# Longer matmul runs in a two-layer transformer trunk: an up projection in runs of 512 columns, a down projection laid out by tokens, and activation slots shifted by 64 and 128 bytes

## The chip, the cores and the metric

The kernel runs on one core of a Trainium2 chip. The metric is the device time of one execution in microseconds (us), lower is better. Engines are named as in the profile: PE (matmul) and PEld (its weight loads), DVE, ACT, POOL, and SP, which issues nearly all DMAs.

## The reference, cut to what matters

Two decoder layers over 256 tokens of width 1024, in float32. The attention half of a layer is a combined projection, three kinds of attention heads, gates and an output projection. The half that the change touches is the MLP at the end of each layer:

```
h = rmsnorm(x, norm_mlp)
x = x + jnp.square(jax.nn.relu(h @ w_up)) @ w_down      # w_up 1024 x 4096, w_down 4096 x 1024
```

After the second layer one more rmsnorm gives the output.

## The kernel before, in words

**Precision.** Every float32 operand of a projection is split into a high part, rounded to the matmul type fp32r, and a low part, the rest. A product a*b is then three matmuls: low weight by high activation, high weight by high activation, high weight by low activation. Weights come as 280 pieces of 128 x 1024 (140 a layer), each by one DMA of 512 KB into a ring `raw` (4 buffers). `split_one` makes the high part (`wh`, ACT, L118) and the low part (`wl`, DVE, L119), six buffers each. `split(n)` also starts the next three pieces, at high priority.

**Layout.** The residual `xres` lies with channels on partitions, [128, 8, 256]: eight channel tiles of 256 tokens. `hilo_slot` gives a 16 KB slot from two that take turns, [128, 2, 8, 256]: eight high tiles, then eight low tiles. It serves as normalized input (`hl`, `xh`), attention output (`oT`) and gated sum (`mg`). `norm_split` (L158 on ACT, L159 on DVE) fills one channel tile of a slot from `xres`; `sumsq` adds its square for the norm. The norm's factor per token is applied after the projections: in the MLP as its square, since relu squared lets it pass through.

**Projection.** `proj` makes 24 matmuls for a 128-wide output tile: for each of eight channel tiles the three products, 256 columns (tokens) each, weights stationary (L198, L199, L200). `v_chunk`, the first work of a layer, is laid out the other way: tokens stationary, 512 weight columns moving (L243 to L245).

**MLP.** 32 hidden tiles of 128 are made in 16 pairs by `up_pair`: two `proj` into the halves of one PSUM bank (`mm`, two buffers), then relu (ACT, L540), square (ACT, L542), high part (DVE copy, L545), low part (DVE, L546) into slots `ga`. The program is written as: pair i of the up projection, then the down products of pair i-1. In the first layer `down(j, d)` multiplies hidden tile j into channel tile d: three matmuls of 256 columns, weights stationary (L557 to L559), for eight d, so 768 matmuls. In the second layer `down_nat(j, t, h)` is laid out by tokens: 128 tokens stationary, 512 weight columns moving, three matmuls (L583 to L585) for four groups (t, h), so 384 matmuls. Both add up in two PSUM tiles `acc2` of two banks each. The last four hidden tiles (TAIL) are kept back and done group by group, so that each group ends apart from the others and its follow-up can start.

**End of the first layer.** For each d: last products, `dve` multiplies by R2 (the squared factor, spread over partitions by `bcast`, L188, and squared at L513), adds to `xres` (L644, L645), then `norm_split` and `sumsq` for the next layer (L168). The next layer's `v_chunk` needs the channel tiles of `hl` one after the other.

**Order.** The Tile framework orders each engine's instructions by a planner that runs its own cost model over the program, so the order on PE follows the program and the priorities only roughly. Attention scores are sent to PE as closed bursts (`burst`, L283). Slots in SBUF follow one another in the order in which their names first occur. Counted from the slots' sizes, `hl`, `ga`, `wh`, `wl` and `V` all lie a multiple of 256 bytes from each other.

Of the kernel before, what the change touches and what calls it, by code (L numbers as in the profile page):

```python
# [30 lines left out]
W_BUFS = 6  # L31
# [7 lines left out]
WK = 5  # L39
# [1 line left out]
START = "w0 x0 w0 x1 w1 x2 w1 x3 w2 x4 x5 w3 x6 x7".split()  # L41
NORM_ACT = False
TAIL = 4
SKEW = 2
# [17 lines left out]
def trunk(ctx: ExitStack, tc: tile.TileContext, w, x, norms, gfin, consts, out):  # L62
# [82 lines left out]
    ident = cst["ident"]  # L145
# [3 lines left out]
    act.activation(tri, tri_raw, AF.Copy)  # L149
    negtri, negones = tri[:, 0], tri[:, 1]  # L150

    def hilo_slot():
        return T("hl", [P, 2, KT, S], 2, F32R)

    def norm_split(hl, nrm, d):

        g = cst["norms"][:, nrm, d:d + 1]
        act.activation(hl[:, 0, d], xres[:, d], AF.Copy, scale=g)  # L158
        dve.scalar_tensor_tensor(hl[:, 1, d], xres[:, d], g, hl[:, 0, d].bitcast(F32),  # L159
                                 op0=ALU.mult, op1=ALU.subtract)  # L160

    def sumsq(d, acc):
# [28 lines left out]
    def proj(dst, n, hl, nk=KT, first=True, last=True, koff=0, woff=0):  # L191

        hi, lo = split(n)
        for k in range(nk):
            c = (woff + k) * P
            a = (first and k == 0)
            z = (last and k == nk - 1)
            pe.matmul(dst, lo[:, c:c + P], hl[:, 0, koff + k], start=a, stop=False, skip_group_check=True)  # L198
            pe.matmul(dst, hi[:, c:c + P], hl[:, 0, koff + k], start=False, stop=False, skip_group_check=True)  # L199
            pe.matmul(dst, hi[:, c:c + P], hl[:, 1, koff + k], start=False, stop=z, skip_group_check=True)  # L200

    acc = T("acc", [P, S], 1)
    hl = hilo_slot()
    for d in range(KT):
        norm_split(hl, 0, d)
        sumsq(d, acc)
# [1 line left out]
    for layer in range(DEPTH):  # L208
        base = layer * PIECES
        xs = hl  # L210
        with tc.high_priority(offset=RPRI):
# [1 line left out]
            Rp = bcast(rcol)  # L213
            R = T("R", [P, S], 1)
            act.activation(R, Rp, AF.Copy)
        xh = hilo_slot()

        def normalized():

            for d in range(KT):  # L220
                t = T("sq", [P, S], 3)
                g = cst["norms"][:, 2 * layer, d:d + 1]
                dve.scalar_tensor_tensor(t, xres[:, d], g, R, op0=ALU.mult, op1=ALU.mult)
                act.activation(xh[:, 0, d], t, AF.Copy)
                dve.tensor_tensor(xh[:, 1, d], t, xh[:, 0, d].bitcast(F32), op=ALU.subtract)


        V = {}
# [1 line left out]
        def v_chunk(c, n):  # L230
            if c == 0:
                pv = [mm_bank(), mm_bank()]
            else:
                sb = s_bank()
                pv = [sb[:, 0], sb[:, 1]]
            for q in range(4):
                hi, lo = split(n + q)
                for kk in range(2):
                    k = 2 * q + kk
                    wsl = slice(kk * 512, kk * 512 + 512)  # L240
                    for t in range(2):
                        tsl = slice(t * P, t * P + P)
                        pe.matmul(pv[t], xs[:, 0, k, tsl], lo[:, wsl], start=k == 0, stop=False)  # L243
                        pe.matmul(pv[t], xs[:, 0, k, tsl], hi[:, wsl], start=False, stop=False)  # L244
                        pe.matmul(pv[t], xs[:, 1, k, tsl], hi[:, wsl], start=False, stop=k == KT - 1)  # L245
# [44 lines left out]
        oT = hilo_slot()  # L290
        last_exp = [None]
        T0, T1, TT = slice(0, P), slice(P, S), slice(0, S)

# [4 lines left out]
            dve.tensor_tensor(oF[j * DH:(j + 1) * DH], po[0:DH, 0:S], tmp, op=ALU.add)  # L298

        def o_split(oF, kt):  # L300
            last_exp[0] = act.activation(oT[:, 0, kt], oF, AF.Copy)
            dve.tensor_tensor(oT[:, 1, kt], oF, oT[:, 0, kt].bitcast(F32), op=ALU.subtract)

        def pv_mm(po, head, kt, ph, pl, first, last):

# [176 lines left out]
                act.preload_act_table_set("natural_log_exp_and_others")  # L482


        mg = hilo_slot()
        for d in range(KT):
            n = base + 60 + d
            st = s_bank()
            sf = st.rearrange("p a b -> p (a b)")
            proj(sf[:, 0:S], n, oT, nk=2, koff=0, woff=0)  # L490
            proj(sf[:, S:2 * S], n, oT, nk=3, koff=2, woff=2)
            proj(sf[:, 2 * S:3 * S], n, oT, nk=3, koff=5, woff=5)
            m3 = T("wk", [P, 3, S], WK)
            m3f = m3.rearrange("p a b -> p (a b)")
            dve.tensor_tensor(m3f, sf[:, 0:3 * S], G[d].rearrange("p a b -> p (a b)"), op=ALU.mult)
            dve.tensor_tensor(m3[:, 0], m3[:, 0], m3[:, 1], op=ALU.add)
            dve.tensor_tensor(m3[:, 0], m3[:, 0], m3[:, 2], op=ALU.add)
            act.activation(mg[:, 0, d], m3[:, 0], AF.Copy)
            dve.tensor_tensor(mg[:, 1, d], m3[:, 0], mg[:, 0, d].bitcast(F32), op=ALU.subtract)


        acc = T("acc", [P, S], 1)
        hl = hilo_slot()
# [46 lines left out]
        def down(j, d):  # L550
            hi, lo = split(npc["d", j])
            uh, ul = us[j // 2]
            a = j == 0 and d < 4
            z = j == 2 * npairs - 1
            dst = down_dst(d)
            c = slice(d * P, d * P + P)
            pe.matmul(dst, lo[:, c], uh[:, j % 2], start=a, stop=False, skip_group_check=True)  # L557
            pe.matmul(dst, hi[:, c], uh[:, j % 2], start=False, stop=False, skip_group_check=True)  # L558
            pe.matmul(dst, hi[:, c], ul[:, j % 2], start=False, stop=z, skip_group_check=True)  # L559

        last = layer == DEPTH - 1
        if last:
# [5 lines left out]
            for t in range(2):  # L568
                for h in range(2):
# [4 lines left out]
            r2 = T("rc", [P, 2], 8)  # L574
            dve.tensor_tensor(r2, rcol, rcol, op=ALU.mult)

        def down_nat(j, t, h):
            hi, lo = split(npc["d", j])
# [5 lines left out]
            pe.matmul(dst, uh[:, j % 2, k], hi[:, c], start=False, stop=False)  # L584
            pe.matmul(dst, ul[:, j % 2, k], hi[:, c], start=False, stop=j == 2 * npairs - 1)  # L585

        groups = [(t, h) for t in range(2) for h in range(2)] if last else [(d,) for d in range(KT)]
        one = down_nat if last else down
        body = 2 * npairs - TAIL
        for i in range(npairs + 1):  # L590
            if i < npairs:
# [40 lines left out]
        hl = hilo_slot()
        for d in range(KT):
            if d == 0:
                for e in range(SKEW):
                    for j in range(body, 2 * npairs - 2):
                        down(j, e)
            if d + SKEW < KT:
# [106 lines left out]
```

## Time and profile before

| what | value |
|---|---|
| time, median of 3 runs | 884.33 us (883.89 to 885.01) |
| time of the profiled execution | 884.33 us |
| its span, first to last instruction | 882.6 us |
| PE busy | 870.9 us, 99% of the span, 6648 matmuls |
| PEld busy | 833.1 us |
| DVE busy | 598.9 us, 68% |
| ACT busy | 494.2 us, 56% |
| granted clock of PE | 0.998 |

A matmul's busy time reaches past the start of the next one, so what one matmul costs in a stream is read from start to start, or from a count of them in a stretch without gaps.

### The profile page before, as it was taken

How to read it: one execution, taken by the hardware profiler on the slowest of the kernel's cores; microseconds unless marked ns; L12 is line 12 of the kernel's file. 1: busy time of each engine (PE TensorE's matmuls, PEld its weight loads, DVE VectorE, ACT ScalarE, POOL GpSimd, SP SyncE). 2: the span in 40 equal slices, each digit the busy share in tenths (PEclk: the TensorE clock that was granted, in tenths of full speed). 3: DMA queues.
4: the chain of work that ended last, by engine and by line, in shares of the span. 5: the costliest groups of instructions: out<-in, count | busy, mean ns of one | idle time of the engine just before them, and what ended most of it. 6: DMA issues, size and time to landing. Idle time of an engine off the chain costs nothing.

```text
span 882.6 us, 16351 instructions
## 1 busy us (share of the span) xinstructions
PE 870.9 (99%) x6648; PEld 833.1 (94%) x6648; DVE 598.9 (68%) x899; ACT 494.2 (56%) x732; POOL 50.7 (6%) x64
## 2 busy tenths in 40 slices
PE   8999999999999999999999999999999999999996
PEld 7899999999999999999988999999999999999995
DVE  6977878855886554555678878787567865555553
ACT  7756566758365444444466664666573554444442
POOL 3000101000030000000020101010000300000000
PEclk9999999999999999999999999999999999999999
DMA  9755443454556666666565554344554666666641
GB/s 316 258 173 159 144 143 121 155 160 151 180 181 186 187 187 181 180 188 184 151 196 187 174 162 142 122 141 146 168 167 145 214 192 191 189 190 187 189 127 48
DMA packets 43562, 151.47 MB, mean 172 GB/s; under 512 B 4960, under 2 KB 6368, under 8 KB 43488
## 3 DMA queue, kind: packets, MB, share of 16 engines
q1 hardware_dynamic: 43056, 149.90, 55.2%
q8 instruction: 52, 0.85, 0.4%
q10 hardware_dynamic: 432, 0.54, 0.2%
q14 instruction: 22, 0.18, 0.1%
HBM read 149.37 MB, written 1.05 MB: 170 GB/s over the span
## 4 chain that ended last, share of the span: by engine, by line
PE 94%; DVE 2%; DMA 1%; issue 1%; ACT 1%; SPq 0%; POOLq 0%; ACTq 0%
PE mm L198 18%; PE mm L199 18%; PE mm L200 18%; PE s L557 4%; PE s L559 4%; PE s L558 3%; PE s L583 3%; PE s L584 3%; PE s L585 3%; PE s L283 2%; PE s L198 2%; PE s L199 2%; PE s L200 2%; PE s L243 2%; PE s L245 2%; PE s L244 2%
## 5 line engine op out<-in xcount | busy, mean ns | idle before, releaser
L119 DVE TENSOR_TENSOR wl<-raw,wh 128x1024 fp32r<-128x1024 f32 (+1 forms) x282 | 343.8, 1222 | 221.7 <-ACT wh L118 221.1
L118 ACT ACTIVATE wh<-raw 128x1024 fp32r<-128x1024 f32 (+1 forms) x282 | 295.0, 1051 | 274.0 <-PE mm L200 151.1
L198 PE MATMUL mm<-hl,wl 128*128 128x256 f32 x1344 | 382.1, 285 | 1.9 <-DVE xres L507 1.9
L199 PE MATMUL mm<-hl,wh 128*128 128x256 f32 x1344 | 381.3, 284 | 0.0
L200 PE MATMUL mm<-hl,wh 128*128 128x256 f32 x1344 | 379.8, 284 | 0.0
L198 PEld LDWEIGHTS mm<-hl,wl 128*128 128x128 f32 x1344 | 257.3, 191 | 3.7 <-DVE xres L507 2.4
L199 PEld LDWEIGHTS mm<-hl,wh 128*128 128x128 f32 x1344 | 257.3, 192 | 0.9
L200 PEld LDWEIGHTS mm<-hl,wh 128*128 128x128 f32 x1344 | 256.7, 191 | 0.3 <-DVE hl L159 0.2
L557 PE MATMUL s<-ga,wl 128*128 128x256 f32 x256 | 72.6, 284 | 0.0
L558 PE MATMUL s<-ga,wh 128*128 128x256 f32 x256 | 72.4, 283 | 0.0
L559 PE MATMUL s<-ga,wh 128*128 128x256 f32 x256 | 72.2, 283 | 0.0
L169 POOL TENSOR_TENSOR acc<-acc,sq 128x256 f32<-128x256 f32 x28 | 26.9, 962 | 417.4 <-ACT sq L168 242.6
L583 PE MATMUL s<-wl,ga 128*128 128x512 f32 x128 | 50.1, 392 | 0.0
L584 PE MATMUL s<-wh,ga 128*128 128x512 f32 x128 | 50.0, 391 | 0.0
L557 PEld LDWEIGHTS s<-ga,wl 128*128 128x128 f32 x256 | 49.1, 192 | 0.4 <-DVE sq L644 0.2
L585 PE MATMUL s<-wh,ga 128*128 128x512 f32 x128 | 49.5, 389 | 0.0
L558 PEld LDWEIGHTS s<-ga,wh 128*128 128x128 f32 x256 | 49.1, 192 | 0.1
L559 PEld LDWEIGHTS s<-ga,wh 128*128 128x128 f32 x256 | 49.0, 192 | 0.2 <-DVE ga L546 0.2
L198 PE MATMUL s<-hl,wl 128*128 128x256 f32 x128 | 36.5, 285 | 0.0
L199 PE MATMUL s<-hl,wh 128*128 128x256 f32 x128 | 36.2, 283 | 0.0
L200 PE MATMUL s<-hl,wh 128*128 128x256 f32 x128 | 36.2, 283 | 0.0
L410 POOL TENSOR_SCALAR_AFFINE_SELECT wk<-wk 128x256 f32<-128x256 f32 x24 | 18.4, 790 | 221.2 <-DVE wk L422 152.2
(132 smaller groups left out, 1124.4 us busy)
## 6 DMA issues: line engine op xcount, KB each, us to landing
raw<-in_w_dram SPq DMA_DIRECT2D x278, 512.0 KB, 4.2
raw<-in_w_dram SPq DMA_DIRECT2D x4, 256.0 KB, 3.5
xres<-in_x_dram SPq DMA_DIRECT2D x8, 128.0 KB, 5.6
wk<-in_gfin_dram SPq DMA_DIRECT2D x2, 256.0 KB, 4.4
out_dram<-V SPq DMA_DIRECT2D x2, 256.0 KB, 2.3
out_dram<-V ACTq DMA_DIRECT2D x2, 256.0 KB, 2.1
c_maskA<-in_maskA_dram SPq DMA_DIRECT2D x1, 384.0 KB, 6.1
c_rope<-in_rope_dram SPq DMA_DIRECT2D x1, 256.0 KB, 5.7
```

The source lines that it names most:

```text
L118: act.activation(hi[:, c:c + step], r[:, c:c + step], AF.Copy)
L119: dve.tensor_tensor(lo[:, c:c + step], r[:, c:c + step], hi[:, c:c + step].bitcast(F32), op=ALU.subtract)
L169: pool.tensor_tensor(acc, acc, sq, op=ALU.add)
L198: pe.matmul(dst, lo[:, c:c + P], hl[:, 0, koff + k], start=a, stop=False, skip_group_check=True)
L199: pe.matmul(dst, hi[:, c:c + P], hl[:, 0, koff + k], start=False, stop=False, skip_group_check=True)
L200: pe.matmul(dst, hi[:, c:c + P], hl[:, 1, koff + k], start=False, stop=z, skip_group_check=True)
L557: pe.matmul(dst, lo[:, c], uh[:, j % 2], start=a, stop=False, skip_group_check=True)
L558: pe.matmul(dst, hi[:, c], uh[:, j % 2], start=False, stop=False, skip_group_check=True)
L559: pe.matmul(dst, hi[:, c], ul[:, j % 2], start=False, stop=z, skip_group_check=True)
L583: pe.matmul(dst, uh[:, j % 2, k], lo[:, c], start=j == 0, stop=False)
L584: pe.matmul(dst, uh[:, j % 2, k], hi[:, c], start=False, stop=False)
L585: pe.matmul(dst, ul[:, j % 2, k], hi[:, c], start=False, stop=j == 2 * npairs - 1)
```

## The change

It has four parts. (1) `hilo_slot(i)` now names its slot, and a slot lies as [128, 8, 2, 256]: of each channel tile the high and the low part side by side, 512 columns in one run. (2) `up_pair` gives each hidden tile a PSUM bank of its own and calls `proj_wide`: eight matmuls of 512 columns (high weight by high and low activation, into the two halves of the bank) and eight of 256 (low weight by high activation). A DVE reduce adds the halves; relu and square become one DVE operation; the high part moves to ACT. (3) The first layer's down projection uses `down_nat`, as the second layer does. At its end each group is scaled on ACT, transposed back by four PE transposes and added to `xres` by one DVE operation; R2 and its broadcast go. (4) The slots are named early, with fillers `skip0` to `skip2`, so that modulo 256 bytes `hl1` lies 64 and `ga` 128 bytes beyond the weights, `hl0` level with them.

```diff
+    for tag, shape, bufs, dt in (("hl0", [P, KT, 2, S], 1, F32R),
+                                 ("skip0", [P, 16], 1, F32),
+                                 ("hl1", [P, KT, 2, S], 1, F32R),
+                                 ("skip1", [P, 16], 1, F32),
+                                 ("ga", [P, 3, S], KT, F32),
+                                 ("skip2", [P, 32], 1, F32),
+                                 ("wh", [P, 1024], W_BUFS, F32R), ("wl", [P, 1024], W_BUFS, F32R), ("V", [P, 2, 8, 2, DH], 3, F32R)):
+        T(tag, shape, bufs, dt)
...
+    def proj_wide(n, hl, bank):
+
+        hi, lo = split(n)
+        for k in range(KT):
+            pe.matmul(bank, hi[:, k * P:k * P + P], hl[:, k].rearrange("p a b -> p (a b)"), start=k == 0, stop=False,
+                      skip_group_check=True)
+        for k in range(KT):
+            pe.matmul(bank[:, 0:S], lo[:, k * P:k * P + P], hl[:, k, 0], start=False, stop=k == KT - 1,
+                      skip_group_check=True)
...
-        if layer < DEPTH - 1:
-            R2 = T("tmp", [P, S], 2)
-            act.activation(R2, bcast(rcol), AF.Square)
...
         def up_pair(i):
-            p = mm_bank()
-            proj(p[:, 0:S], npc["u", 2 * i], hl)
-            proj(p[:, S:2 * S], npc["u", 2 * i + 1], hl)
-            s1 = T("wk", [P, 512], WK)
-            act.activation(s1, p, AF.Relu)
-            u = T("wk", [P, 512], WK)
-            act.activation(u, s1, AF.Square)
+            t = T("wk", [P, 2, S], WK)
+            for a in range(2):
+                p = mm_bank()
+                proj_wide(npc["u", 2 * i + a], hl, p)
+                dve.tensor_reduce(t[:, a], p.rearrange("p (a b) -> p b a", a=2), axis=mybir.AxisListType.X, op=ALU.add)
+            u = T("wk", [P, 2, S], WK)
+            dve.scalar_tensor_tensor(u, t, 0.0, t, op0=ALU.max, op1=ALU.mult)
             uh = T("ga", [P, 2, S], KT, F32R)
             ul = T("ga", [P, 2, S], KT, F32R)
-            dve.tensor_copy(uh.rearrange("p a b -> p (a b)"), u)
-            dve.tensor_tensor(ul.rearrange("p a b -> p (a b)"), u, uh.rearrange("p a b -> p (a b)").bitcast(F32), op=ALU.subtract)
+            act.activation(uh, u, AF.Copy)
+            dve.tensor_tensor(ul, u, uh.bitcast(F32), op=ALU.subtract)
...
-        groups = [(t, h) for t in range(2) for h in range(2)] if last else [(d,) for d in range(KT)]
-        one = down_nat if last else down
+        groups = [(t, h) for t in range(2) for h in range(2)] if last else [(t, h) for h in range(2) for t in range(2)]
+        one = down_nat
...
-            tmp = T("sq", [P, S], 3)
-            dve.tensor_tensor(tmp, down_dst(d), R2, op=ALU.mult)
-            dve.tensor_tensor(xres[:, d], xres[:, d], tmp, op=ALU.add)
-            norm_split(hl, 2 * layer + 2, d)
-            sumsq(d, acc)
+            y = T("wk", [P, 512], WK)
+            act.activation(y, acc2[h][:, t], AF.Copy, scale=r2[:, t:t + 1])
+            tb = t_bank()
+            for d in range(4):
+                pe.transpose(tb[:, d * P:(d + 1) * P], y[:, d * P:(d + 1) * P], ident)
+            x4 = xres[:, 4 * h:4 * h + 4, t * P:(t + 1) * P]
+            dve.tensor_tensor(x4, x4, tb.rearrange("p (a b) -> p a b", a=4), op=ALU.add)
+            if t == 1:
+                for d in range(4 * h, 4 * h + 4):
+                    norm_split(hl, 2 * layer + 2, d)
+                    sumsq(d, acc)
```

## Rows read from the trace of the kernel before

**Rows 1.** Page, part 1 and part 2: busy time by engine, clock by slice.

```profile
PE 870.9 (99%) x6648; PEld 833.1 (94%) x6648; DVE 598.9 (68%) x899; ACT 494.2 (56%) x732; POOL 50.7 (6%) x64
...
PEclk9999999999999999999999999999999999999999
```

**Rows 2.** Page, part 4: the chain that ended last, by engine.

```profile
PE 94%; DVE 2%; DMA 1%; issue 1%; ACT 1%; SPq 0%; POOLq 0%; ACTq 0%
```

**Rows 3.** Windows: the first layer's MLP, all matmuls 256 columns wide; busy (x started).

```profile
274.00:434.00 160.00, 160.00 (x1336) 160.00 (x1335) 82.19 (x83) 74.34 (x84) 0.00 (x0) 1.00 0.63 185
```

**Rows 4.** Timeline of PE, second layer: from 256 columns to 512 and back.

```profile
740.99 0.28 PE L200 MATMUL mm<-hl,wh 128*128 128x256 f32 x1
741.11 0.40 PE L583 MATMUL s<-wl,ga 128*128 128x512 f32 x1
...
742.50 0.39 PE L583 MATMUL s<-wl,ga 128*128 128x512 f32 x1
...
746.58 0.28 PE L198 MATMUL mm<-hl,wl 128*128 128x256 f32 x1
746.69 0.28 PE L199 MATMUL mm<-hl,wh 128*128 128x256 f32 x1
746.81 0.28 PE L200 MATMUL mm<-hl,wh 128*128 128x256 f32 x1
```

**Rows 5.** Chain in order of time: start, length; transposes, and R2's broadcast.

```profile
268.07 0.43 PE t L188 x2
...
702.48 0.44 PE t L572 x4
```

**Rows 6.** Groups in the first layer's MLP on DVE and ACT (count, busy, mean ns).

```profile
L119 DVE TENSOR_TENSOR wl<-raw,wh 128x1024 fp32r<-128x1024 f32 x56 | 68.6, 1225 | 77.4 <-ACT wh L118 77.4
L546 DVE TENSOR_TENSOR ga<-wk,ga 128x512 fp32r<-128x512 f32 x14 | 9.7, 693 | 0.5
L545 DVE CAST ga<-wk 128x512 fp32r<-128x512 f32 x13 | 5.5, 426 | 0.0
...
L118 ACT ACTIVATE wh<-raw 128x1024 fp32r<-128x1024 f32 x56 | 59.3, 1059 | 85.9 <-PE mm L200 48.2 <-PE s L559 37.0 <-DVE ga L545 0.7
L542 ACT ACTIVATE wk<-wk 128x512 f32<-128x512 f32 x14 | 8.9, 633 | 0.4
L540 ACT ACTIVATE wk<-mm 128x512 f32<-128x512 f32 x14 | 8.1, 581 | 0.0
```

**Rows 7.** Groups of the whole span: operations nearest to the new ones.

```profile
L268 DVE TENSOR_TENSOR qk<-mm,c_rope 128x512 f32<-128x512 f32 x18 | 12.1, 673 | 0.0
L250 ACT ACTIVATE V<-s,rc 128x512 fp32r<-128x512 f32 x8 | 5.4, 677 | 0.6 <-DVE V L251 0.5
...
L618 DVE SCALAR_TENSOR_TENSOR V<-s,rc,V 128x512 f32<-128x512 f32 x4 | 3.0, 748 | 3.8 <-PE s L585 3.8
```

**Rows 8.** Groups at the first layer's end, 434 to 450 us.

```profile
L119 DVE TENSOR_TENSOR wl<-raw,wh 128x1024 fp32r<-128x1024 f32 x4 | 5.4, 1352 | 1.7 <-ACT wh L118 1.7
L559 PEld LDWEIGHTS s<-ga,wh 128*128 128x128 f32 x26 | 4.9, 191 | 0.2 <-DVE ga L546 0.2
...
L557 PEld LDWEIGHTS s<-ga,wl 128*128 128x128 f32 x25 | 4.8, 190 | 0.4 <-DVE sq L644 0.2
...
L159 DVE SCALAR_TENSOR_TENSOR hl<-xres,c_norms,hl 128x256 fp32r<-128x256 f32 x5 | 3.1, 620 | 0.4 <-ACT hl L158 0.4
...
L158 ACT ACTIVATE hl<-xres,c_norms 128x256 fp32r<-128x256 f32 x6 | 3.0, 501 | 4.6 <-DVE xres L645 4.6
...
L168 ACT ACTIVATE sq<-xres 128x256 f32<-128x256 f32 x5 | 2.0, 402 | 0.0
```

More of the change, by code (lines that the diff above doesn't have):

```diff
@@ L43 @@
 TAIL = 4
-SKEW = 2
 UNIT_RATE = {"v": 2, "qk": 1, "g": 2}
@@ L150, in trunk, with hilo_slot @@
     negtri, negones = tri[:, 0], tri[:, 1]
-    def hilo_slot():
-        return T("hl", [P, 2, KT, S], 2, F32R)
+    def hilo_slot(i):
+        return T("hl%d" % i, [P, KT, 2, S], 1, F32R)
     def norm_split(hl, nrm, d):
         g = cst["norms"][:, nrm, d:d + 1]
-        act.activation(hl[:, 0, d], xres[:, d], AF.Copy, scale=g)
-        dve.scalar_tensor_tensor(hl[:, 1, d], xres[:, d], g, hl[:, 0, d].bitcast(F32),
+        act.activation(hl[:, d, 0], xres[:, d], AF.Copy, scale=g)
+        dve.scalar_tensor_tensor(hl[:, d, 1], xres[:, d], g, hl[:, d, 0].bitcast(F32),
                                  op0=ALU.mult, op1=ALU.subtract)
@@ L197, in proj @@
             z = (last and k == nk - 1)
-            pe.matmul(dst, lo[:, c:c + P], hl[:, 0, koff + k], start=a, stop=False, skip_group_check=True)
-            pe.matmul(dst, hi[:, c:c + P], hl[:, 0, koff + k], start=False, stop=False, skip_group_check=True)
-            pe.matmul(dst, hi[:, c:c + P], hl[:, 1, koff + k], start=False, stop=z, skip_group_check=True)
+            pe.matmul(dst, lo[:, c:c + P], hl[:, koff + k, 0], start=a, stop=False, skip_group_check=True)
+            pe.matmul(dst, hi[:, c:c + P], hl[:, koff + k, 0], start=False, stop=False, skip_group_check=True)
+            pe.matmul(dst, hi[:, c:c + P], hl[:, koff + k, 1], start=False, stop=z, skip_group_check=True)
+    def proj_wide(n, hl, bank):
[6 more added lines that the diff above has]
+                      skip_group_check=True)
     acc = T("acc", [P, S], 1)
-    hl = hilo_slot()
+    hl = hilo_slot(0)
     for d in range(KT):
@@ L215, in trunk @@
             act.activation(R, Rp, AF.Copy)
-        xh = hilo_slot()
+        xh = hilo_slot(1)
         def normalized():
@@ L223, in normalized @@
                 dve.scalar_tensor_tensor(t, xres[:, d], g, R, op0=ALU.mult, op1=ALU.mult)
-                act.activation(xh[:, 0, d], t, AF.Copy)
-                dve.tensor_tensor(xh[:, 1, d], t, xh[:, 0, d].bitcast(F32), op=ALU.subtract)
+                act.activation(xh[:, d, 0], t, AF.Copy)
+                dve.tensor_tensor(xh[:, d, 1], t, xh[:, d, 0].bitcast(F32), op=ALU.subtract)
         V = {}
@@ L242, in v_chunk @@
                         tsl = slice(t * P, t * P + P)
-                        pe.matmul(pv[t], xs[:, 0, k, tsl], lo[:, wsl], start=k == 0, stop=False)
-                        pe.matmul(pv[t], xs[:, 0, k, tsl], hi[:, wsl], start=False, stop=False)
-                        pe.matmul(pv[t], xs[:, 1, k, tsl], hi[:, wsl], start=False, stop=k == KT - 1)
+                        pe.matmul(pv[t], xs[:, k, 0, tsl], lo[:, wsl], start=k == 0, stop=False)
+                        pe.matmul(pv[t], xs[:, k, 0, tsl], hi[:, wsl], start=False, stop=False)
+                        pe.matmul(pv[t], xs[:, k, 1, tsl], hi[:, wsl], start=False, stop=k == KT - 1)
             V[c] = T("V", [P, 2, 8, 2, DH], 3, F32R)
@@ L288, in burst @@
                     before = i
-        oT = hilo_slot()
+        oT = hilo_slot(0)
         last_exp = [None]
@@ L300, in o_split @@
         def o_split(oF, kt):
-            last_exp[0] = act.activation(oT[:, 0, kt], oF, AF.Copy)
-            dve.tensor_tensor(oT[:, 1, kt], oF, oT[:, 0, kt].bitcast(F32), op=ALU.subtract)
+            last_exp[0] = act.activation(oT[:, kt, 0], oF, AF.Copy)
+            dve.tensor_tensor(oT[:, kt, 1], oF, oT[:, kt, 0].bitcast(F32), op=ALU.subtract)
         def pv_mm(po, head, kt, ph, pl, first, last):
@@ L482, in trunk @@
                 act.preload_act_table_set("natural_log_exp_and_others")
-        mg = hilo_slot()
+        mg = hilo_slot(1)
         for d in range(KT):
@@ L497, in trunk @@
             dve.tensor_tensor(m3[:, 0], m3[:, 0], m3[:, 2], op=ALU.add)
-            act.activation(mg[:, 0, d], m3[:, 0], AF.Copy)
-            dve.tensor_tensor(mg[:, 1, d], m3[:, 0], mg[:, 0, d].bitcast(F32), op=ALU.subtract)
+            act.activation(mg[:, d, 0], m3[:, 0], AF.Copy)
+            dve.tensor_tensor(mg[:, d, 1], m3[:, 0], mg[:, d, 0].bitcast(F32), op=ALU.subtract)
         acc = T("acc", [P, S], 1)
-        hl = hilo_slot()
+        hl = hilo_slot(0)
         for d in range(KT):
@@ L535, in up_pair @@
         def up_pair(i):
-            p = mm_bank()
-            proj(p[:, 0:S], npc["u", 2 * i], hl)
-            proj(p[:, S:2 * S], npc["u", 2 * i + 1], hl)
-            s1 = T("wk", [P, 512], WK)
-            act.activation(s1, p, AF.Relu)
-            u = T("wk", [P, 512], WK)
-            act.activation(u, s1, AF.Square)
+            t = T("wk", [P, 2, S], WK)
[5 more added lines that the diff above has]
+            dve.scalar_tensor_tensor(u, t, 0.0, t, op0=ALU.max, op1=ALU.mult)
             uh = T("ga", [P, 2, S], KT, F32R)
             ul = T("ga", [P, 2, S], KT, F32R)
-            dve.tensor_copy(uh.rearrange("p a b -> p (a b)"), u)
-            dve.tensor_tensor(ul.rearrange("p a b -> p (a b)"), u, uh.rearrange("p a b -> p (a b)").bitcast(F32), op=ALU.subtract)
+            act.activation(uh, u, AF.Copy)
+            dve.tensor_tensor(ul, u, uh.bitcast(F32), op=ALU.subtract)
             us[i] = (uh, ul)
[L550 to L559, printed above, removed]
         last = layer == DEPTH - 1
@@ L573, in trunk @@
                     dve.tensor_copy(xn[t][h], tb)
-            r2 = T("rc", [P, 2], 8)
-            dve.tensor_tensor(r2, rcol, rcol, op=ALU.mult)
+        r2 = T("rc", [P, 2], 8)
+        dve.tensor_tensor(r2, rcol, rcol, op=ALU.mult)
         def down_nat(j, t, h):
@@ L631, in trunk @@
         acc = T("acc", [P, S], 1)
[L632 to L638, printed above, removed]
+        hl = hilo_slot(0)
+        for i, (t, h) in enumerate(groups):
+            if i == 0:
                 for j in range(body, 2 * npairs - 2):
-                    down(j, d + SKEW)
+                    one(j, t, h)
+            if i + 1 < len(groups):
+                for j in range(body, 2 * npairs - 2):
+                    one(j, *groups[i + 1])
             for j in range(2 * npairs - 2, 2 * npairs):
-                down(j, d)
-            tmp = T("sq", [P, S], 3)
-            dve.tensor_tensor(tmp, down_dst(d), R2, op=ALU.mult)
-            dve.tensor_tensor(xres[:, d], xres[:, d], tmp, op=ALU.add)
-            norm_split(hl, 2 * layer + 2, d)
-            sumsq(d, acc)
+                one(j, t, h)
+            y = T("wk", [P, 512], WK)
[9 more added lines that the diff above has]
+                    sumsq(d, acc)
 def constants():
```

2 lines of the change are left out of this document (removed).

## The prediction

> **What bounds the kernel now.** The page comes first: PE is busy 99% of the span and its clock is granted in full in all 40 slices, the higher of its two levels, 2.4 GHz [rows 1]. The chain that ended last confirms it: 94% of it is PE [rows 2]. So a microsecond that PE saves is a microsecond of the kernel, as long as no other engine fills the gap, and the question for every edit is what PE pays for it. Since a matmul's busy time overlaps the next one, I read prices from counts and starts. The windows view has a stretch of the first layer's MLP in which PE never stops: 1336 matmuls of 256 columns in 160.00 us, 119.8 ns each [rows 3]. The timeline of PE in the second layer has eighteen matmuls of 512 columns between 742.50 and 746.58: 4.08 / 18 = 226.7 ns each [rows 4]. Two of 256 columns cost 239.6 ns, so a joined one saves 12.9 ns. At 2.4 GHz the columns alone take 106.7 and 213.3 ns; what is left is 13 ns for a matmul of either width. A matmul has a fixed price, and the change makes fewer of them.
>
> **Change of width.** The same timeline shows one more price. The first six matmuls of 512 columns after a run of 256 take 742.50 - 741.11 = 1.39 us, where six at the steady pace take 1.36; the first of 256 after 512 takes 0.11, not 0.12 [rows 4]. There and back costs 0.03 - 0.01 = 0.02 us.
>
> **Up projection.** A hidden tile has 24 matmuls of 256 columns, 24 x 119.8 = 2875 ns. It gets eight of 512 and eight of 256, 8 x 226.7 + 8 x 119.8 = 2772 ns. The saving is 103 ns, for 32 tiles in two layers 64 x 103 = 6.6 us.
>
> **First down projection.** 768 matmuls of 256 columns become 384 of 512: 92.0 - 87.05 = 5.0 us saved.
>
> **Changes of width, counted.** Each up tile now ends in 256 columns and is followed by 512: 64 in two layers. Before, the first layer's MLP had none and the second's one per pair, 16. 48 more at 0.02 us cost 1.0 us.
>
> **Transposes and R2.** The first layer's end gets 16 transposes on PE. The nearest are the second layer's own: four in 0.44 us [rows 5], so 4 x 0.44 = 1.8 us. R2's broadcast goes, two passes of 0.43 us [rows 5] that stood in PE's stream: -0.4 us.
>
> A rule of the Trainium skill speaks against the main term: TensorE: Matmul & The Clock Gate, section Back-to-back issue gap, gives a warm isolated matmul its columns at the clock plus 2.5 ns. By it a joined run would save 2.5 ns and the 512 + 384 joins 2.2 us in place of 11.6 us, which the transposes nearly use up. The rows differ, 119.8 and 226.7 ns against 109.2 and 215.8 ns [rows 3, 4], and where they differ I go by the rows.
>
> **DVE and ACT.** In the stretch of rows 3 DVE is busy 82.19 of 160 us, 51%. A pair takes 96 x 0.1198 = 11.5 us there, so 5.9 us of DVE. The edit takes away a copy of 0.43 us [rows 6] and adds two reduces that read 512 columns of PSUM and one operation over 512 in SBUF. No row shows a reduce, nor a read that jumps between two halves of a bank. The nearest, 512 from PSUM, takes 0.67 us, the other some 0.75 [rows 7]. DVE gets 5.9 - 0.4 + 1.3 + 0.75 = 7.6 us in a period that falls to 2 x 2.77 + 24 x 0.2267 + 0.04 = 11.0 us: 69%, hidden under PE. The cover is gone when a reduce takes (11.0 - 5.9 + 0.4 - 0.75) / 2 = 2.4 us, over three times the nearest row; at that point the cost starts from nothing, so I put it at nothing. ACT loses relu and square, 0.58 + 0.63 us, and gets one copy of about 0.63 [rows 6]. A bank of `mm` is now filled by one tile; the next tile to want it is two later, past one tile (2.8 us) and, after the first pair, 24 down matmuls (5.4 us), while the reduce and a `wl` of 1.23 us queued ahead of it need 1.9.
>
> **Where a wait may come.** At two places PE has little cover. First, after the last up pair of each layer PE has twelve matmuls left that don't need it, 2.7 us. The new chain is end of matmul 0.28, reduce 0.67, relu and square 0.75, copy 0.63: 2.3 us to `uh`, 3.0 to `ul`, which is used third, at 3.2 us. It just fits; a `wl` in the queue in front costs up to 1.2 us, twice. Before, such waits cost 0.2 and 0.4 us [rows 8]. Second, the hand-over to the next layer. After the last group: scaling 0.68, transposes 0.44 with 0.27 to the end, addition 0.67 [rows 7], `norm_split` 0.50 and 0.62 [rows 8]: some 3.2 us until channel tile 4 is there. Each later tile waits for another 0.50 + 0.40 us of ACT [rows 8]. What covers it is `v_chunk` on channel tiles 0 to 3, which need only the first two groups: 24 x 0.2267 = 5.4 us. If the planner spends that work earlier, PE waits up to 3.2 us. Nothing lost is one end, 2.4 + 3.2 = 5.6 us the other; the rows before stand near the first end, so I take 0.5 us.
>
> **Slots.** In the kernel before all matmul operands lie whole multiples of 256 B apart, so no row prices 64 or 128 B. Moved are `hl1`, the moving side of q, k, gates (48 tiles a layer) and output projection (8 tiles): 2 x 56 x 24 = 2688 matmuls; and `ga`, stationary in 768. Bounds for these 3456: a gain of the whole fixed part, 13 ns each, 45 us; a loss like that of the first six after a change of width, 0.03 / 6 = 5 ns each, 17 us. Since the fixed part is the same at 256 and 512 columns, it doesn't grow with what is streamed, as a clash of addresses would. I take zero.
>
> The Trainium skill, SBUF — State Buffer, section SBUF: two separate sides, lists GpSimd's shared port and the DMA ports as the only places of contention; no run here shows that, and by it the slots change nothing.
>
> **Sum.** -6.6 - 5.0 + 1.0 + 1.8 - 0.4 + 0.5 = -8.7 us. The profiled execution took 884.33 us, 1.7 beyond its span, and is the median itself: 875.6 us.
>
> **Rivals.**
> (a) The slots help as well: 1 to 4 ns on 3456 matmuls, 3.5 to 14 us, 862 to 872 us. For it: the fixed 13 ns has no explanation in the profile. Against: the argument above.
> (b) The slots hurt, in the stages of q, k, gates and output projection that the other parts don't touch. From 8.7 / 3456 = 2.5 ns a matmul it eats the gain, from 3.0 ns the kernel is slower than 886.1; at the 5 ns bound it is 875.6 + 17 = 893 us. Only the missing row speaks for it.
> (c) Joining doesn't pay here. In a run of eight, most matmuls are among the first six, and if the fixed part belonged to the weights' side of the stream rather than to each matmul, two times 256 and one 512 would be equal: 884.33 + 1.8 - 0.4 + 0.5 = 886 us. With only the up runs affected the down projection's 5.0 remain: 881. Say 884. The steady 226.7 ns speak against. The Trainium skill's rule on the back-to-back gap (TensorE: Matmul & The Clock Gate), quoted above, is on this side.
> (d) The gain stands but the ends lose: both waits at their bound, 3 to 5.6 us, 878.5 to 881 us. For it: serial chains with thin cover, and an order that the planner sets anew. Against: before, PE waits there under 1 us.
>
> **Chances.** Forecast 0.65, its own range 873 to 878.5; (a) 0.13; (b) 0.08; (c) 0.06; (d) 0.08. A measurement of this kernel can tell about 0.2% from no change, 1.8 us: 882.6 to 886.1. Faster: the forecast, (a), and 0.07 of (d), 0.85. Same: (c) and a remainder of (d), 0.07. Slower: (b), 0.08. For eight in ten, 866 to 881 leaves out (b), (c) and the far third of (a), 0.18.
>
> **What would show it.** Right: a period of a pair at 11.0 us in both layers (before, 96 x 0.1198 = 11.5 in the first, 48 x 0.1198 + 24 x 0.2267 + 0.02 = 11.2 in the second); 512-column matmuls at 0.227, with six of some 0.23 at the start of each run; a reduce near 0.7 us; DVE about 70% busy in the MLP; PE's idle time at the first layer's end under 1 us; gate and output projections still at 119.8 ns. Wrong: another price for the 256-column matmuls on `hl1`, at once (a) or (b); 512-column matmuls of 0.235 or more throughout a run, (c); PE waiting for `xres`, `hl` or `ga` at the ends, (d).

## The result, and the profile after

The changed kernel takes 877.75 us (median of 4 runs, 876.88 to 878.69) where the kernel before took 884.52 beside it: a ratio of 0.9924 (95% interval 0.9907 to 0.9941, in brackets from here on), 6.8 us faster. The forecast was 875.6.

The page after, parts 1 and 4, answers to [rows 1] and [rows 2]: 882 matmuls fewer, DVE 44 us busier, PE still the engine that sets the end.

```profile
PE 860.6 (98%) x5766; PEld 780.7 (89%) x5766; DVE 643.2 (73%) x950; ACT 477.1 (54%) x703; POOL 50.8 (6%) x64
...
PE 90%; DVE 4%; ACT 2%; issue 2%; DMA 1%; SPq 0%; POOLq 0%; ACTq 0%; DVEq 0%
```

The windows view of the first layer's MLP answers to [rows 3]: PE never stops, and DVE is busy 102.61 of 156 us, 66%.

```profile
274.00:430.00 156.00, 156.00 (x781) 131.59 (x780) 102.61 (x112) 65.71 (x69) 0.00 (x0) 1.00 0.58 189
```

In its groups, the reduce and the joined relu and square:

```profile
L553 DVE TENSOR_REDUCE wk<-mm 128x256 f32<-128x512 f32 x28 | 19.4, 692 | 18.4 <-PE mm L218 18.4
...
L555 DVE SCALAR_TENSOR_TENSOR wk<-wk 128x512 f32<-128x512 f32 x14 | 9.6, 684 | 0.0
```

The chain (start, length) has one line per run of eight 512-column matmuls, two a pair; from pair to pair it is 11.17 us, where 11.0 was forecast:

```profile
285.68 1.84 PE mm L215 x8
...
296.85 1.84 PE mm L215 x8
...
308.01 1.84 PE mm L215 x8
```

Most of the difference lies in the down projection. In PE's timeline its 24 matmuls take 430.68 - 425.11 = 5.57 us, 232.1 ns each. The 24 of [rows 4], the dearer first six included, took 746.58 - 741.11 = 5.47 us, 227.9 ns each:

```profile
425.11 0.39 PE L584 MATMUL s<-wl,ga 128*128 128x512 f32 x1
...
430.68 0.39 PE L584 MATMUL s<-wl,ga 128*128 128x512 f32 x1
```

And outside the MLP, where no matmul was joined, a projection on `hl1` goes faster. From 472.85 to 484.04 the timeline has 95 steps of 256 columns on end, 11.19 / 95 = 117.8 ns, not the 119.8 of [rows 3]:

```profile
472.85 0.28 PE L207 MATMUL mm<-hl,wl 128*128 128x256 f32 x1
...
484.04 0.28 PE L209 MATMUL mm<-hl,wh 128*128 128x256 f32 x1
```

PE's waits (in total, times, longest) show three lines at the MLP's two ends:

```profile
PE mm L215 <- DVE hl L168: 2.0, 2, 1.0
PE mm L215 <- DVE xres L526: 1.9, 2, 1.0
...
PE t L647 <- ACT wk L644: 0.8, 1, 0.8
```

The wait on `xres` stood there before (1.9 us); the first is new, one in each layer, and so is the last, in the hand-over. In PE's timeline both waits on L215 fall at the start of the MLP, not at its tail:

```profile
254.37 1.31 PE L215 MATMUL mm<-hl,wh 128*128 128x512 f32 x5
256.71 0.50 PE L215 MATMUL mm<-hl,wh 128*128 128x512 f32 x1 [1.03 <-DVE hl L168]
...
258.18 2.10 PE L215 MATMUL mm<-hl,wh 128*128 128x512 f32 x8 [0.96 <-DVE xres L526]
```

DVE's timeline has what PE waits for: a channel tile of `hl`, and an addition to `xres` that stands behind a split of weights (`wl`):

```profile
255.71 0.95 DVE L168 SCALAR_TENSOR_TENSOR hl<-xres,c_norms,hl 128x256 fp32r<-128x256 f32 x1
256.58 1.21 DVE L128 TENSOR_TENSOR wl<-raw,wh 128x1024 fp32r<-128x1024 f32 x1
257.72 0.41 DVE L526 TENSOR_TENSOR xres<-xres,mm 128x256 f32<-128x256 f32 x1
```

So by the trace: -6.6 and -5.0 for fewer matmuls, +1.0 for changes of width, +1.8 for transposes and -0.4 for R2 stand as forecast. To these come 2688 x (117.6 - 119.8) ns = -5.9 us on `hl1`, 768 x (232.2 - 227.9) ns = +3.3 on `ga`, 448 x 2 ns = +0.9 since 512 columns in the up runs average 230.7 (228.8 without the change's distances), +2.4 that PE stands longer at the two MLP starts (from the starts of its matmuls), +0.45 for the hand-over, and about +0.5 at the kernel's start. The sum is -7.6; the spans differ by 6.9, so 0.7 us is left over.

### The profile page after: what moved, and what is told of

The parts are those of the page before. It is cut to its first block, busy times and chain, and to the rows that moved or that the text cites. A ratio compares the mean times of both kernels' runs of the same rounds, so it can differ in the third digit from the quotient of the medians.

```text
span 875.7 us, 14658 instructions
## 1 busy us (share of the span) xinstructions
PE 860.6 (98%) x5766; PEld 780.7 (89%) x5766; DVE 643.2 (73%) x950; ACT 477.1 (54%) x703; POOL 50.8 (6%) x64
## 4 chain that ended last, share of the span: by engine, by line
PE 90%; DVE 4%; ACT 2%; issue 2%; DMA 1%; SPq 0%; POOLq 0%; ACTq 0%; DVEq 0%
PE mm L215 13%; PE mm L207 10%; PE mm L208 10%; PE mm L209 10%; PE mm L218 7%; PE s L586 7%; PE s L584 7%; PE s L585 7%; PE s L302 2%; DVE wl L128 2%; PE s L262 2%; PE s L264 2%; PE s L263 2%; PE s L207 1%; PE s L209 1%
## 5 line engine op out<-in xcount | busy, mean ns | idle before, releaser
L128 DVE TENSOR_TENSOR wl<-raw,wh 128x1024 fp32r<-128x1024 f32 (+1 forms) x282 | 342.5, 1218 | 118.6 <-ACT wh L127 117.8
L207 PE MATMUL mm<-hl,wl 128*128 128x256 f32 x832 | 234.2, 282 | 0.0
L208 PE MATMUL mm<-hl,wh 128*128 128x256 f32 x832 | 233.2, 281 | 0.0
L209 PE MATMUL mm<-hl,wh 128*128 128x256 f32 x832 | 232.2, 280 | 0.0
L207 PEld LDWEIGHTS mm<-hl,wl 128*128 128x128 f32 x832 | 156.3, 188 | 0.8
L208 PEld LDWEIGHTS mm<-hl,wh 128*128 128x128 f32 x832 | 156.2, 188 | 0.3
L209 PEld LDWEIGHTS mm<-hl,wh 128*128 128x128 f32 x832 | 155.9, 188 | 0.0
L215 PE MATMUL mm<-hl,wh 128*128 128x512 f32 x512 | 130.2, 394 | 4.0 <-DVE hl L168 2.0
L215 PEld LDWEIGHTS mm<-hl,wh 128*128 128x128 f32 x512 | 93.8, 188 | 24.3 <-DVE hl L168 2.9
L584 PE MATMUL s<-wl,ga 128*128 128x512 f32 x256 | 101.2, 395 | 0.0
L585 PE MATMUL s<-wh,ga 128*128 128x512 f32 x256 | 100.9, 394 | 0.0
L586 PE MATMUL s<-wh,ga 128*128 128x512 f32 x256 | 100.4, 395 | 0.0
L218 PEld LDWEIGHTS mm<-hl,wl 128*128 128x128 f32 x512 | 69.9, 190 | 5.0
L553 DVE TENSOR_REDUCE wk<-mm 128x256 f32<-128x512 f32 x64 | 44.2, 691 | 40.1 <-PE mm L218 40.0
L218 PE MATMUL mm<-hl,wl 128*128 128x256 f32 x512 | 71.5, 282 | 0.0
L586 PEld LDWEIGHTS s<-wh,ga 128*128 128x128 f32 x256 | 48.1, 188 | 11.1
L584 PEld LDWEIGHTS s<-wl,ga 128*128 128x128 f32 x256 | 48.3, 189 | 10.2 <-DVE V L619 0.4
L585 PEld LDWEIGHTS s<-wh,ga 128*128 128x128 f32 x256 | 48.2, 188 | 9.8
```

The lines of the kernel that those rows point to most:

```text
L128: dve.tensor_tensor(lo[:, c:c + step], r[:, c:c + step], hi[:, c:c + step].bitcast(F32), op=ALU.subtract)
L207: pe.matmul(dst, lo[:, c:c + P], hl[:, koff + k, 0], start=a, stop=False, skip_group_check=True)
L208: pe.matmul(dst, hi[:, c:c + P], hl[:, koff + k, 0], start=False, stop=False, skip_group_check=True)
L209: pe.matmul(dst, hi[:, c:c + P], hl[:, koff + k, 1], start=False, stop=z, skip_group_check=True)
L215: pe.matmul(bank, hi[:, k * P:k * P + P], hl[:, k].rearrange("p a b -> p (a b)"), start=k == 0, stop=False, skip_group_check=True)
L218: pe.matmul(bank[:, 0:S], lo[:, k * P:k * P + P], hl[:, k, 0], start=False, stop=k == KT - 1, skip_group_check=True)
```

## The experiments

"Distance" below is the byte address of the operand that streams (or, where activations are stationary, lies loaded) against the weights, modulo 256; "level" is 0. The weights never move modulo 256, so a distance is an address of the activations as well. A price is the mean distance from start to start of consecutive matmuls, worked out from all their starts in a trace. The first theory (S): a constant distance changes what every matmul costs. Its rival (O): it doesn't, and the missing part comes from the order of the work and its waits.

**1. `level`: the change without its distances.**

```diff
-                                 ("skip0", [P, 16], 1, F32),
-                                 ("skip1", [P, 16], 1, F32),
-                                 ("skip2", [P, 32], 1, F32),
```

> The changed kernel without the three fillers: hl0, hl1 and ga all lie a multiple of 256 B from the weights. Theory S (the distance in bytes between the operand that streams and the one that is loaded sets a part of each matmul's price): the 2688 matmuls on hl1 go back from 117.6 to 119.8 ns (+5.9 us) and the 768 with ga stationary from 232.2 to 226.7 ns (-4.2 us): 877.75 + 1.7 = 879.4 us. Theory O (order and stage, not bytes, make the differences): 877.8 us, and both prices stay at 117.6 and 232.2.

Measured 878.87 us (877.87 to 880.59), 0.9936 [0.9921, 0.9951]: near S's 879.4. In the same stretch as above, 95 steps take 485.67 - 474.27 = 11.40 us, 120.0 ns:

```profile
474.27 0.28 PE L204 MATMUL mm<-hl,wl 128*128 128x256 f32 x1
...
485.67 0.28 PE L206 MATMUL mm<-hl,wh 128*128 128x256 f32 x1
```

So the change without its distances is worth 5.8 us. The distances, a gain and a loss together, come to 1.1, which the runs alone don't tell from nothing (877.87 to 880.59 against 876.88 to 878.69); the prices in the traces do.

**2. `ga_level`: `hl1` at 64 B, `ga` level.**

```diff
-                                 ("skip1", [P, 16], 1, F32),
+                                 ("skip1", [P, 48], 1, F32),
...
-                                 ("skip2", [P, 32], 1, F32),
```

> The changed kernel with ga level with the weights and hl1 still 64 B beyond. S: only the 768 matmuls with ga stationary change, 232.2 to 226.7 ns: 877.75 - 4.2 = 873.5 us, a pair of the MLP in 11.04 instead of 11.17 us. O: 877.8 us, 11.17 us.

Measured 874.81 us (874.02 to 875.53), 0.9886 [0.9869, 0.9902]: nearer to S's 873.5 than to O's 877.8, and the 128 B under `ga` cost 2.9 us. The down projection returns to 227.9 ns, and the chain's pair to 297.36 - 286.33 = 11.03 us, the forecast's 11.0:

```profile
286.33 1.81 PE mm L214 x8
...
297.36 1.81 PE mm L214 x8
```

**3. `slots_only`: the kernel before with the change's slots, nothing joined.** Slots get the names and fillers of the change; layout and matmuls stay those of before.

```diff
+    for tag, shape, bufs, dt in (("hl0", [P, 2, KT, S], 1, F32R),
+                                 ("skip0", [P, 16], 1, F32),
...
-        return T("hl", [P, 2, KT, S], 2, F32R)
+        return T("hl%d" % i, [P, 2, KT, S], 1, F32R)
```

> The kernel before with the slots of the change alone (hl1 64 B, ga 128 B beyond the weights), all matmuls in their old widths. S: hl1 gives -5.9 us, ga as stationary operand in the second layer 384 x 5.5 ns = +2.1 us; ga as moving operand in the first layer is unknown, between -2.2 and +5.5 ns on 768 matmuls (-1.7 to +4.2 us): 884.5 - 3.8 = 880.7, between 879 and 885 us. O: 884.5 us.

Measured 880.39 us (880.14 to 880.82), 0.9952 [0.9937, 0.9967]. S again (880.7): `hl1` 117.6 ns, `hl0` 119.8, `ga` streaming at 128 B 118.7, `ga` stationary 232.2.

**4. `scan`: many distances in one kernel.** 32 B behind each channel tile and each `ga` buffer, so that the distance steps through 0 to 224 B from tile to tile.

```diff
-        return T("hl%d" % i, [P, KT, 2, S], 1, F32R)
+        return T("hl%d" % i, [P, KT, 2 * S + 8], 1, F32R)[:, :, 0:2 * S].rearrange("p k (a b) -> p k a b", a=2)
```

> The changed kernel with 32 B of padding behind each channel tile of hl0 and hl1 and behind each of the eight ga buffers, so that the eight lie 0, 32, 64 ... 224 B beyond the weights, all in one run. S: the price of a matmul goes with the tile: on hl1 119.8 ns at 0 B and 117.6 at 64 B, with ga stationary 226.7 at 0 B and about 232 at 128 B, and the other six distances show where the best lies. O: no dependence on the tile within a stage, differences under 0.5 ns.

One run, 881.82 us, slower than `level`. Where the distance changes every few matmuls, 256 columns cost some 117 to 119 ns, but 512 with `ga` stationary 231 to 235 whatever the distance, level ones 232 too. So the expectation that level ones keep 226.7 missed: by this one run the price goes with the matmuls around as well, not with the single one alone.

**5 and 6. `steps1`, `steps2`: one constant distance per use and layer.** Each activation slot is 256 B larger and its view is shifted inside it.

```diff
+OFF = {'v': (64, 192), 'xh': (128, 192), 'oT': (160, 224), 'mg': (32, 96), 'up': (64, 128), 'ga': (64, 192)}
...
+    def shifted(t, n, off):
+        return t[:, off // 4:off // 4 + n]
+
+    def hilo_slot(i, off):
+        t = shifted(T("hl%d" % i, [P, KT * 2 * S + 64], 1, F32R), KT * 2 * S, off)
+        return t.rearrange("p (k a b) -> p k a b", k=KT, a=2)
```

`steps2` has OFF = {'v': (32, 128), 'xh': (32, 96), 'oT': (64, 128), 'mg': (160, 224), 'up': (192, 32), 'ga': (32, 96)}.

> The changed kernel with one constant distance for each use of a slot, to measure further distances at a steady pace. Bytes beyond the weights: v_chunk 64 and 192 (first and second layer), q, k and gates 128 and 192, attention output 160 and 224, output projection 32 and 96, up projection 64 and 128, ga 64 and 192. Theory S1 (a constant distance gives a constant price, and 64 B is good for every moving operand): the up projection at 64 B pays about 2 to 4 ns less than level in both widths, q, k and gates at 128 and 192 B lie between 112 and 124 ns, each with a spread of under 3 ns. Theory S2 (the good 64 B is an accident of that stage): the up projection at 64 B pays 119.9 and 226.9 ns as when level. No forecast for the whole time, since the distances are mixed: 870 to 885 us.

> As the run beside it, with other distances: v_chunk 32 and 128 B, q, k and gates 32 and 96, attention output 64 and 128, output projection 160 and 224, up projection 192 and 32, ga 32 and 96. S1: attention output at 64 B pays 117.6 ns where level it paid 119.9; a distance gives the same price in each 256-column stage. S2: attention output at 64 B pays 119.9. Whole time 870 to 885 us.

One run each, 876.77 and 882.21 us. Prices in ns, runs 1, 2 and 5 filling in level and 64 B:

| distance, B | 0 | 32 | 64 | 96 | 128 | 160 | 192 | 224 |
|---|---|---|---|---|---|---|---|---|
| 256 columns, activations streaming | 119.8 | 117.0 | 117.6 | 119.7 | 119.0 | 117.8 | 114.5 to 115.5 | 118.2 |
| 512 columns in the up runs | 228.8 | 233.0 | 231.8 | | 232.7 | | 232.6 | |
| 512 columns, `ga` stationary | 227.9 | 233.1 | 233.3 | 234.2 | 232.2 | | 229.5 | |

The first theory's half on narrow matmuls held, its half on wide ones fell: for 256 columns level and 96 B are the dearest distances and 192 B the cheapest; for 512 level is the cheapest of all. What is best for the wide matmul is worst for the narrow one, and the change's 128 B under `ga`, stationary for 512, is on the wrong side.

**7 and 8. `up_only`, `down_only`: half of the joining each, all level.** The first keeps the down projection of before, with R2 and its end; the second the up projection of before.

```diff
 # up_only
-        one = down_nat
+        one = down_nat if last else down
 # down_only
-                proj_wide(npc["u", 2 * i + a], hl, p)
+            proj(p[:, 0:S], npc["u", 2 * i], hl)
+            proj(p[:, S:2 * S], npc["u", 2 * i + 1], hl)
```

> Up projection in runs of 512 columns alone: slots level, first down projection and its hand-over as before. By the prediction's terms with the waits that the changed kernel's trace showed: -6.6 (joined runs) + 1.0 (changes of width) + 2.4 (two more waits at the start of the MLP) = -3.2: 881.4 us. Rival (the waits at the MLP's start come from the new down projection's order, not from the up projection): 879.0 us, no wait of more than 1.3 us in all at either start.

> First down projection in tokens alone: slots level, up projection in 256 columns as before. By the prediction's terms: -5.0 + 1.8 (transposes) - 0.4 (R2) + 0.3 (sixteen changes of width) + 0.8 (wait at the hand-over, as in the changed kernel) = -2.5: 882.1 us. Rival (the hand-over costs nothing more than before): 881.3 us.

`up_only` 882.61 us (880.88 to 884.83), 0.9978 [0.9969, 0.9988]; `down_only` 881.91 (881.31 to 882.15), 0.9969 [0.9957, 0.998]. The forecast had -5.6 and -3.6 us (-6.6 + 1.0; -5.0 + 1.8 - 0.4); they are -2.0 and -2.7 (together 4.7, where `level` has 5.8; the intervals cover the difference). PE's waits say which half brings the wait on `hl`; first `up_only`:

```profile
PE mm L213 <- DVE xres L524: 1.9, 2, 1.0
PE mm L213 <- DVE hl L166: 1.3, 2, 0.8
```

and `down_only`, which has none on `hl` from DVE and alone of the two has the hand-over's:

```profile
PE mm L204 <- DVE xres L523: 1.6, 2, 0.8
...
PE t L644 <- ACT wk L641: 0.8, 1, 0.8
```

The waits seem to have a second price. In the trace of `up_only` PE's granted clock falls to 1.2 GHz, its lower level, for 3.4 us at both MLP starts, 0.1 and 1.3 us after PE's two waits of about 1 us each there have ended. This is the first (the 0.51 is the mean granted clock, as a share of 2.4 GHz):

```profile
260.90:264.40 3.50, 3.50 (x10) 2.74 (x10) 2.29 (x3) 0.74 (x2) 1.13 (x1) 0.51 0.83 229
```

Matmuls of 512 columns start 427 ns apart in it, so eight of them lose 8 x (427 - 229) ns = 1.6 us. It doesn't come in each execution. The ten of `up_only` sort by their mean granted clock: 880.88 to 882.02 us at 0.999 (three), 882.15 to 882.78 at 0.996 or 0.997 (five), 884.45 and 884.83 at 0.994. A fall of 3.4 us to half the clock takes 0.002 off an execution's mean, so the three at 0.999 have none; they average 881.4, the expectation's number, and the clock accounts for its miss of 1.2 us. Such falls, one or two of 3.4 us or one of 6.8, stand at the MLP's start in the traces of `level`, `ga_level`, `steps2`, `best_after`, `best_before` and `s_banks` too. The traces of before, `slots_only`, `down_only` and `best_s` have none before the kernel's last microseconds, and nor has the kept trace of the changed kernel, although it has the waits; but its four executions are at 0.998, 0.998, 0.996 and 0.996 and took 877.4, 876.88, 878.1 and 878.69 us. So every fall follows waits at the MLP's start, and not every wait brings one.

**9 and 10. `best_after`, `best_before`: each kernel at its best distances.** The change with 192 B where 256 columns stream (`xh`, `oT`, `mg`), level elsewhere; and the kernel before, nothing joined, with 192 B under everything that streams 256 columns (the up projection and the first layer's `ga` too).

```diff
 # best_after
+OFF = {'v': (0, 0), 'xh': (192, 192), 'oT': (192, 192), 'mg': (192, 192), 'up': (0, 0), 'ga': (0, 0)}
 # best_before
-        hl = hilo_slot()
+        hl = hilo_slot(0, 192)
...
+            uh, ul = (shifted(T("ga", [P, 3 * S], KT, F32R), 2 * S, 0 if layer else 192).rearrange("p (a b) -> p a b", a=2)
+                      for _ in range(2))
```

> The changed kernel with the distance that measured best in each use: 192 B for the slots that move in 256 columns (q, k and gates, attention output, output projection), level for all that takes part in matmuls of 512. From the run with all slots level, 878.9, less 3072 matmuls x 4.3 ns (119.8 to 115.5) = 13.2: 865.7 us. Rival (the cheap 192 B needs its stage to be the only one of that distance, or the weights' split becomes the bound): over 870 us.

> The kernel before, all its matmuls in the old widths, with 192 B for every moving slot (also up projection and the first layer's ga), level for v_chunk and the second layer's ga. 5376 matmuls x 4.3 ns = 23.1: 884.5 - 23.1 = 861.4 us, faster than the changed kernel at its best distances, since 24 x 115.5 = 2772 ns for an up tile is less than 8 x 226.8 + 8 x 119.8 + 30 = 2803. Rival (256 columns at 192 B can't hold that pace over the MLP, where the splits fill more of DVE): 867 us or more, joined runs stay ahead.

`best_after` 868.87 us (868.56 to 869.19), 0.9821 [0.9807, 0.9836]; `best_before` 864.0 (863.53 to 865.64), 0.977 [0.9755, 0.9784]. Without a single joined matmul the kernel before beats the changed one by 13.7 us, and the change's best version here by 4.9. The first layer's MLP in `best_before`, the window that answers to [rows 3], 120 / 1062 = 113.0 ns:

```profile
300.00:420.00 120.00, 120.00 (x1062) 120.00 (x1061) 65.70 (x67) 59.38 (x67) 0.00 (x0) 1.00 0.65 195
```

At that price two matmuls of 256 columns cost what one of 512 costs at its best, 226.7, and a hidden tile's 24 cost 2.71 us against 8 x 228.8 + 8 x 118.9 = 2.78 with joined runs (level, where narrow matmuls between wide ones average 118.9). But 192 B is no single price. In the timeline of `best_before` 48 steps from 406.84 take 5.44 us, 113.3 ns, and 95 steps from 463.44 take 11.19, 117.8 ns, at the same distance:

```profile
406.84 0.28 PE L210 MATMUL mm<-hl,wh 128*128 128x256 f32 x1
...
412.28 0.28 PE L569 MATMUL s<-ga,wh 128*128 128x256 f32 x1
...
463.44 0.28 PE L208 MATMUL mm<-hl,wl 128*128 128x256 f32 x1
...
474.63 0.28 PE L210 MATMUL mm<-hl,wh 128*128 128x256 f32 x1
```

Whole stretches run at one of these two levels; the means near 115 in the table are mixtures. In `best_before` the second layer's MLP, with 512 columns between, runs at the dear level throughout. The expectations miss by some 3 us each, but not by having taken one price: the mean over the narrow matmuls at 192 B is 115.2 ns in `best_before` and 114.9 in `best_after`, under the 115.5 that they took. What they left out are waits and the clock: it falls once in the trace of `best_before` and twice in that of `best_after`, at the MLP's start. In `best_after` the wait on `hl` has also grown, since PE arrives earlier:

```profile
PE mm L217 <- DVE hl L170: 2.9, 2, 1.4
```

**11 and 12. `s_banks`, `best_s`: the waits at the MLP's start.** The last odd tile of the output projection holds a bank of `mm` until DVE has added it to `xres`. Here it is moved to the idle `s` banks, in `ga_level` and in `best_before`:

```diff
-            p = mm_bank() if d % 2 else t_bank()
+            p = s_bank()[:, 0] if d % 2 else t_bank()
```

> The run with ga level (874.81 us), with the odd tiles of the output projection in the s banks, which are idle then, so that the up projection finds both mm banks free. Theory B (at the start of the MLP the second up tile waits for a bank that the addition to xres frees late, 1.9 us of PE's waits in two layers, and the wait for hl is a consequence): the wait on xres goes, PE fills the wait for hl with the second tile, 2 to 4 us less: 871 to 873 us. Rival H (the last channel tile of hl comes late, DVE being full in that stretch; the bank only hides it): the wait moves to hl, 874 to 875 us.

> The same edit in the fastest version so far (864.0 us; the kernel before in old widths with 192 B under every moving slot), which waits 1.7 us for xres and 0.9 for hl at the two starts. B: 862 us. H: 864 us.

`s_banks` 875.94 us (874.41 to 876.53), 0.9898 [0.9884, 0.9913], no gain over `ga_level`. The wait on `xres` is gone, the one on `hl` stays, and one on the norm's sum of squares takes the other's place:

```profile
PE mm L214 <- DVE hl L167: 2.1, 2, 1.1
PE t L183 <- POOL acc L177: 2.0, 2, 1.0
```

`best_s` 859.68 us (858.77 to 859.94), 0.9714 [0.9698, 0.973], is the fastest version, 24.8 us below the kernel before. With narrow tiles the wait on `xres` was the one that held PE: no wait on `xres` or `hl` is left at the MLP's start, and the sum of squares costs

```profile
PE t L185 <- POOL acc L179: 0.7, 2, 0.4
```

It gained 4.3 us over `best_before`, more than the waits removed (1.7 + 0.9 - 0.7 = 1.9). Some of the rest is the level of the second layer's gate stage: 113.3 ns there (640 to 660 us) in place of 117.8, for some 170 matmuls, 0.8 us, of which the next 10 us give back 0.3. Most of the remainder is the clock. In the trace of `best_before` it falls after the waits of the second layer, and nine steps of 256 columns take 680.09 - 678.17 = 1.92 us, 213.3 ns each:

```profile
677.80:681.30 3.50, 3.50 (x19) 3.50 (x18) 1.40 (x2) 0.00 (x0) 1.12 (x1) 0.51 0.79 255
```

```profile
678.17 0.41 PE L208 MATMUL mm<-hl,wl 128*128 128x256 f32 x1
...
680.09 0.41 PE L208 MATMUL mm<-hl,wl 128*128 128x256 f32 x1
```

Sixteen such steps lose 16 x (213.3 - 117.8) ns = 1.5 us. The trace of `best_s` has no such fall, and its four executions are at 0.997 to 0.999 where those of `best_before` are at 0.994 to 0.997. Together 1.9 + 0.5 + 1.5 = 3.9 of the 4.3 us.

## Why the prediction was right, and where it was not

**Direction and range: right. Main mechanism: right at level distance and full clock.** A joined matmul saves nearly what [rows 3] and [rows 4] say, 226.7 to 228.9 for 512 columns against 2 x 119.8, with all slots level; of the 8.7 us forecast for it with its transposes and waits `level` gives 5.8; waits and clock took the rest, as far as it is traced (below). The Trainium skill's rule on the back-to-back gap (TensorE: Matmul & The Clock Gate, section Back-to-back issue gap), which the page gives for an isolated matmul and by which joining gives next to nothing, does not hold for this stream: `level` gains 5.8 us. With it fell rival (c), at the distances of this kernel; at 192 B its equality, two narrow for one wide, holds. Nor is the price of 13 ns one that every matmul has, as the prediction concluded: at 1.2 GHz 256 and 512 columns start 213.3 and 427 ns apart, which is what the columns alone take at that clock.

**Reduce, DVE, ACT: right.** 0.69 us where 0.67 was taken, DVE at 66% for 69%, hidden under PE.

**The step that failed is the slots, "I take zero".** Its argument was that a fixed part of 13 ns, equal at 256 and 512 columns, can't depend on addresses. It does: distance alone moves the narrow matmul between 119.8 and 113.3 ns, and the wide one with `ga` stationary between 227.9 and 234.2. That the fixed parts were equal belongs to the level distance. Rival (a) had the sign for `hl1` (2.2 ns, in its 1 to 4), rival (b) that for `ga` (4.3 ns, under its bound of 5); together they nearly cancel, -5.9 against 3.3 + 0.9 = 4.2 us, so it is luck that a wrong step left the sum almost right. The Trainium skill (SBUF — State Buffer, section SBUF: two separate sides) names GpSimd's shared port and the DMA ports as the places of contention; by it runs 1 to 3 would not differ in price, and `ga_level` against `level`, 0.9886 to 0.9936, disagrees.

**Waits: right place for one, the other not seen.** The hand-over waits 0.94 us in all, close to the 0.5 taken above what was there. At the MLP's tail PE waits less than 1 us. But the prediction didn't look at the MLP's start. There the first wide tile eats eight channel tiles in 1.8 us, so it runs into those still in DVE's queue behind additions and `wl`, where three narrow products each spread it over 2.9 us; and a second tile now needs a bank of its own while the output projection still holds it. That is +2.4 us, and `up_only` shows that it comes with the up runs. `s_banks` shows that the bank alone isn't it: DVE's chain behind the last output tile is late for either.

**Clock: left out.** The prediction read a clock granted in full before [rows 1] and took it for the kernel after. With the longer waits it falls in some executions, at some 1.6 us a fall: the changed kernel's two executions at 0.996 are 1.3 us above its two at 0.998, and of the 3.6 us that `up_only` lacks 2.4 are put down to the waits and 1.2 to the clock. What decides whether a wait brings a fall, these runs don't show.

**Short up runs.** Eight wide matmuls on end average 228.8 at level, since the first after narrow ones are dearer, as [rows 4] had it; over 512 of them 2 ns are the 1.0 us that the change of width was put at. With the change's distances they average 230.7.

**Open.** Why the price follows the distance, why wide and narrow matmuls want opposite ones, why it has two levels at 192 B and what picks between them isn't settled: no run separates the streamed operand from the weight load or the PSUM write, nor the distance to the weights from the activations' own address, since the weights stayed in place modulo 256 B; and distances were told apart only modulo 256 B in steps of 32. That the part beyond the columns is gone at 1.2 GHz says only that it doesn't simply add to them.

## What to carry to other kernels

Where PE runs without gaps, read the price of a matmul from start to start, then move an operand by some tens of bytes and read it again: 192 B under the narrow matmuls were worth 20 us here, over three times the joining, and cost no instruction. Don't give one offset to all: an operand that is stationary for 512 columns wanted 0. And when a matmul is widened, look where the operand that it eats is still being made; the gain is lost there first, once as a wait and in some executions again as a lower clock behind it. Before a remainder of 1 or 2 us is put down to the kernel, set the executions beside their granted clocks.

## What the runs showed of the hardware that was not expected

- 256 columns cost 119.8 ns at distance 0, 117.6 at 64 B, and 113.3 or 117.8, in long stretches of either, at 192 B; the columns alone are 106.7 ns at the granted 2.4 GHz.
- 512 columns cost 226.7 at distance 0 once steady (227.9 over runs of 24), and 229 to 234 at every other distance tried.
- After waits at the MLP's start the granted clock falls, in some executions, to 1.2 GHz for 3.4 us (6.8 in one); 256 and 512 columns then cost 213.3 and 427 ns, the columns alone.
- Distances that change from matmul to matmul make 512 columns dear (231 to 235 ns with `ga` stationary, in one run), level ones included.
- A DVE reduce that adds two halves of a PSUM bank takes 0.69 us, where a plain operation over 512 columns there takes 0.67 [rows 7].
